# Fetching cache pages with direct transfers on SP's queue, addressed from registers, in place of indirect transfers on POOL's

## The chip, the cores and the metric

The kernel runs on one core of one Trainium2 chip. The metric is the device time of one execution in microseconds (us). A core has five engines that run side by side, each through its own queue of instructions in order: PE (TensorE, matrix products; its weight loads are shown as PEld), DVE (VectorE), ACT (ScalarE), POOL (GpSimd) and SP (SyncE, which here only issues transfers). All transfers run on the same 16 DMA engines.

## The reference, cut to what matters

One decoder layer serves a prompt (512 positions) and eight samples (8 new positions each, 1024 cached ones) with the same weights.

```python
z = rmsnorm(x) @ w_in                      # q, k/v streams, window k/v, gates, gMLP
# mixer A: three attention branches, gated and summed
kc, vc = compress_blocks(k_cmp), compress_blocks(v_cmp)   # a small MLP over blocks of 32 keys, stride 16
o = g0 * attend(q, kc, vc) + g1 * attend(q, selected 64-key blocks) + g2 * attend(q, last 512 keys)
# mixer B: u * (W_s v + b) in chunks of 128
x = x + [A ; B] @ w_out
x = x + relu(rmsnorm(x) @ w_ff1)**2 @ w_ff2
```

For the samples the past keys and values come out of a paged cache: `past = cache_kv[l][page_table]`. A page holds 128 positions; each sample has 8 pages, so the table has 64 entries, a permutation of pages in a pool of 80. Streams 0 and 1 (`k_cmp`, `v_cmp`) go into the compression, streams 2 and 3 into the selected-block branch.

## The kernel before, in words

The host lays the cache out as two arrays, `cache_kv` (compression streams) and `cache_slc` (selected streams), each with 128 rows of 256 floats per page: one page of either is 128 KB, one row of 1 KB for each of the 128 partitions.

The stages follow each other in the text of `_body`:

1. Norm and transposes of the input, then the whole projection by `w_in` for prompt and samples (`tok_mm`, `q_piece`), with the compression of the prompt's keys and the gMLP in between. The last projection product ends near 153 us, the gelu behind it near 170 us.
2. The prompt's attention (`prompt_attention`, lines 718 to 738): eight blocks of (key head, query tile), four heads each, so 32 steps. `head_scores` makes three score products per head and their maxima (DVE, line 672) and exponentials (ACT, line 673); `head_scales` normalises; `values` of the block before (transposes `tp`, line 703, copies `ptf`, products `o`) is interleaved. Beside it runs the compression of the samples' cached keys: from step 5 on, every third step, one of the eight tasks of lines 743 to 747 is emitted: `compress_keys(pr)` and `compress_values(pr)` for the four pairs of samples `pr`. Each calls `hidden`, 32 products of `w1` with the pages in `Gc[pr]`, written to `pcs`.
3. The samples' attention (`soft`, `values`, from line 777), which reads the pages in `Gs[pr]`, interleaved with the output projection (`out_proj`).
4. Norm, then the feed-forward layers over `w_ff1` and `w_ff2` (from line 1009) and the last norm.

The pages are fetched by `gather` (line 581): 16 pages for a pair of samples, one indirect transfer per page on POOL's queue, with row numbers out of `idx`, an integer tile made from the page table at lines 338 to 343 (table entry times 128 plus the partition's number). There are four fetches for `Gc` and four for `Gs`, 128 pages in all. `Gc` has two buffers (`gc_`, line 575), so `Gc[2]` and `Gc[3]` wait until the products on `Gc[0]` and `Gc[1]` are done; `load_cmp(pr + 2)` stands in `compress_values`, line 639. `Gs[0]` and `Gs[1]` have buffers of their own beside them; `Gs[2]` and `Gs[3]` (lines 768 to 770) take the place of `w1` and `Gc` once these are closed (line 749). The memory of all these tiles was the projection's, and comes free between 153 and 170 us.

SP issues every other load and store: in stage 2 the `VB` rows (577, 578), the window keys `KW` (595, two buffers), window values `W` (600) and `w1` (576); later the weights for the output projection and the feed-forward layers (`load_unit`, line 139).

The order on each engine's queue isn't that of the text alone. A scheduler simulates the program over time and puts each instruction on its engine's queue when its operands and its buffer are free in that simulation (line 1125, `schedule_with_timeline_sim`). On the chip a queue is then strictly in order: an instruction that waits holds all behind it on the same engine. In the trace POOL's order was 27 pages of `Gs[0]` and `Gs[1]`, then `Gc[0]` and `Gc[1]` whole, then the last 5 of `Gs[1]`, later `Gc[2]`, `Gc[3]`, `Gs[2]`, `Gs[3]`.

Of the kernel before, what the change touches and what calls it, by code (L numbers as in the profile page):

```python
# [11 lines left out]
F32 = mybir.dt.float32  # L12
F32R = mybir.dt.float32r
BF = mybir.dt.bfloat16
I32 = mybir.dt.int32
AF = mybir.ActivationFunctionType
ALU = mybir.AluOpType
# [14 lines left out]
def _build_consts():  # L32
    p = np.arange(128)
    blocks = []
    kept = ("ident", "gsum", "iota16", "valid0")

    def add(name, a):
        a = np.asarray(a, np.float32)
        full = np.zeros((128, a.shape[1]), np.float32)
        full[: a.shape[0]] = a  # L40
        blocks.append((name not in kept, name, full))

    add("ident", np.eye(128))
    add("causal", np.where(p[None, :] <= p[:, None], 0.0, NEG))
    n = np.arange(32)
    cm = [np.where(16 * n[None, :] + 31 <= (128 * i + p)[:, None], 0.0, NEG) for i in range(4)]
    add("cmpmask", np.concatenate(cm, 1))
    q = p % 8
    sm = np.zeros((128, 584), np.float32)
    sm[:, 63] = NEG  # L50
    sm[:, 64:72] = np.where(np.arange(8)[None, :] <= q[:, None], 0.0, NEG)
    c = np.arange(512)
    key = 4 * (c % 128) + c // 128
    sm[:, 72:] = np.where(key[None, :] >= q[:, None] + 1, 0.0, NEG)
    add("winmask", sm)
    add("newmask", np.where(np.arange(8)[None, :] <= q[:, None], 0.0, NEG))
    add("tril", (p[None, :] <= p[:, None]).astype(np.float32))
    seq, hh, gg = p // 64, (p % 64) // 32, (p % 32) // 8
    add("gsum", ((seq[:, None] == seq[None, :]) & (hh[:, None] == hh[None, :]) & (q[:, None] == q[None, :])))
    add("iota16", np.broadcast_to(np.arange(16), (128, 16)))  # L60
    add("headsel", ((hh * 4 + gg)[:, None] == np.arange(8)[None, :]))
    tok = np.arange(64)
    sel = [((tok // 8)[:, None] == (2 * pr + seq)[None, :]) & ((tok % 8)[:, None] == q[None, :]) for pr in range(4)]
    add("gatesel", np.concatenate(sel, 1))
    add("pageoff", p[:, None])
    add("rep8", (np.arange(8)[:, None] == (tok % 8)[None, :]))
    add("bdiag", (tok // 8)[:, None] == np.arange(8)[None, :])
    add("valid0", (p >= 31)[:, None])
    blocks.sort(key=lambda b: b[0])
    o = 0  # L70
    for _, name, a in blocks:
        _CONSTS[name] = (o, a.shape[1])
        o += a.shape[1]
    return np.concatenate([b[2] for b in blocks], 1), sum(b[2].shape[1] for b in blocks if not b[0])


CONST_ARRAY, NKEEP = _build_consts()
NCONST = CONST_ARRAY.shape[1]

# [5 lines left out]
def body(tc, I, O):  # L85
    nc = tc.nc
    ctx = ExitStack()
    with ctx:
        _body(ctx, tc, nc, I, O)


def _body(ctx, tc, nc, I, O):
    act, dve, pool, pe, sp = nc.scalar, nc.vector, nc.gpsimd, nc.tensor, nc.sync
# [22 lines left out]
    def C(name, rows=128):  # L116
        o, w = _CONSTS[name]
        return cst[:rows, o:o + w] if o < NKEEP else cst2_[0][:rows, o - NKEEP:o - NKEEP + w]
# [67 lines left out]
    samp = ctx.enter_context(tc.tile_pool(name="samp", bufs=1, side="right"))  # L186
# [4 lines left out]
    b2c = samp.tile([128, 2], F32, name="b2c")  # L191
    b2r = samp.tile([128, 2, 64], F32, name="b2r")
    b1p = samp.tile([128, 2, 2], F32, name="b1p")
    idx = samp.tile([128, 64], I32, name="idx")

    cot = ctx.enter_context(ExitStack())
    OTp = cot.enter_context(tc.tile_pool(name="otp", bufs=1, side="right")).tile([128, 8, NP], F32, name="OTp")
# [55 lines left out]
    early = ccs.enter_context(tc.tile_pool(name="early", bufs=1, side="right", reuse_waits="tile"))  # L253
# [54 lines left out]
    with ExitStack() as c4:  # L308
# [15 lines left out]
        for t in range(5):  # L324
            if t:
                norm_transpose(n1, pst, "tr", x[t][:tsz[t]], t, g1, AH, AL, AST)
            p = psm.tile([128, 512], F32, name="pd", tag="mm")
# [6 lines left out]
        pool.tensor_copy(dst, C(name))  # L334

    ptt = early.tile([128, 64], I32, name="ptt")
    pt = I["page_table"]
    sp.dma_start(ptt, bass.AP(tensor=pt.tensor, offset=pt.offset, ap=[[0, 128], [1, 64]]))  # L340
    ptf = early.tile([128, 64], F32, name="ptf")
    dve.tensor_copy(ptf, ptt)
    dve.tensor_scalar(idx, ptf, 128.0, C("pageoff"), op0=ALU.mult, op1=ALU.add)


    b1c = early.tile([128, 2], F32, name="b1c")
# [38 lines left out]
    for st in range(2):  # L385
        x_ = cp.tile([128, 8, 66], F32, name=f"X{st}")
        p = pst.tile([128, 512], F32, name="pkc", tag="tr")
# [41 lines left out]
    with ExitStack() as c4:  # L429
# [14 lines left out]
        for g2 in range(2):  # L444
            p = pst.tile([128, 4, 128], F32, name="pws", tag="tr")
# [12 lines left out]
        for t, p in enumerate(vps):  # L458
            rows = tsz[t]
            if t == 4:  # L460
                tmp = halves(p, 512)
                p = ev.tile([64, 512], F32, name="zg", tag="z")
# [8 lines left out]
                                     op0=ALU.subtract, op1=ALU.mult)  # L471
# [5 lines left out]
        p = pst.tile([128, 2, 64], F32, name="pkn", tag="tr")  # L477
# [4 lines left out]
        for g in range(0, 8, 2):  # L482
            p = pst.tile([128, 2, 4, 64], F32, name="psg", tag="tr")
# [4 lines left out]
        p = pst.tile([64, 8, 64], F32, name="psgs", tag="tr")  # L488
# [41 lines left out]
    for m in range(4):  # L530
        if m % 2 == 0:
            us = [load_pair(m * 128, i, pool) for i in range(4)]
        for half in range(2):
            p = psm.tile([128, 512], F32, name="pq", tag="mm")
# [5 lines left out]
    for t, p in enumerate(tok_mm(1304, 512)):  # L540
        rows = tsz[t]
        if t == 4:
# [3 lines left out]
            p = z  # L546
        u = uw.tile([128, 512], F32, name="u", tag="u", bufs=2)
        gelu(nc, uw, p, 512, None, None, out=u[:rows], rows=rows, times=S[:rows, t])
        p = pst.tile([128, 4, 128], F32, name="pob", tag="tr")
# [9 lines left out]
    with ExitStack() as c4:  # L559
# [20 lines left out]

        def gather(dst, src, pr):
            for j in range(16):
                pool.indirect_dma_start(out=dst[:, j], out_offset=None, in_=src,  # L583
                                        in_offset=bass.IndirectOffsetOnAxis(ap=idx[:, pr * 16 + j:pr * 16 + j + 1], axis=0))

        Gc = {}

        def load_cmp(pr):
            Gc[pr] = gc_[pr % 2].tile([128, 16, 256], F32, name="Gc", tag="Gc")
            gather(Gc[pr], I["cache_kv"], pr)  # L590
# [37 lines left out]
        def compress_values(pr):  # L628
            gel = hidden(pr, 1)
            pv = psf.tile([64, 2, 2, 64], F32, name="pv2", tag="fill")  # L630
            for sq in range(2):
                for h in range(2):
                    f = sq == 0 and h == 0
                    mm(pv[:, sq, h, :], gel[:, (h * 2 + sq) * 64:(h * 2 + sq) * 64 + 64], w2z[:, 1, 64:128],
                       f, True, f)
            dve.tensor_tensor(VB[0:64, pr].rearrange("p s (h d) -> p (s h) d", h=2),
                              pv.rearrange("p s h d -> p (s h) d"), bcast(b2r[0:64, 1], [[0, 4], [1, 64]]), op=ALU.add)
            if pr < 2:
                load_cmp(pr + 2)
            if pr == 1:  # L640
                gather(Gs[1], I["cache_slc"], 1)
# [98 lines left out]
        load_cmp(0)  # L740
        load_cmp(1)
        gather(Gs[0], I["cache_slc"], 0)
        tasks = [(f, pr) for pr in range(4) for f in (compress_keys, compress_values)]
        for i, _ in enumerate(prompt_attention()):
            if i >= 5 and i % 3 == 2 and tasks:
                f, pr = tasks.pop(0)
# [382 lines left out]
```

## Time and profile before

| | us |
|---|---|
| median of 3 runs | 998.38 (997.47 to 1001.69) |
| the profiled execution's own time | 999.24 |
| its span in the trace | 997.5 |

| engine | busy us | share of the span |
|---|---|---|
| PE | 833.1 | 84% |
| PEld | 688.7 | 69% |
| DVE | 429.8 | 43% |
| ACT | 344.8 | 35% |
| POOL | 228.6 | 23% |

The DMA engines moved 90.2 MB: 72.55 MB on the hardware queue (SP's transfers, 23.2% of the 16 engines' span) and 16.85 MB on the software queue (POOL's, 5.8%). The mean granted TensorE clock was 0.906 of full speed.

How to read such a profile: a row of a group or of the timeline gives the engine, the line of the kernel, the operation, the tile written and the tiles read. The bracket behind it is the time for which the engine stood idle before, and what is inferred to have ended that: an instruction, a transfer, "issue" (the engine waited for nothing that the profile shows) or "remote", which is the same as "another core or an unknown queue" in the chain (a signal whose sender the profile doesn't show). The shares of busy time are averages over stages with different limits, so a change in one stage is read from that stage.

### The profile page before, as it was taken

The numbers are of one execution on the slowest core, as the hardware profiler recorded it, in microseconds if no ns is written. First come the engines' busy times: TensorE is split into PE (matmuls) and PEld (weight loads), VectorE is DVE, ScalarE is ACT, GpSimd is POOL, SyncE is SP. The second block draws the span as 40 slices with busy tenths as digits, with TensorE's granted clock in tenths as the row PEclk, the third lists the DMA queues.
The fourth block names the chain that finished last, engine by engine and source line by source line (L and its number), as shares of the span: only waits on it lengthen the run. The fifth ranks groups of instructions, "written<-read, shape, count | busy, mean of one in ns | idle before, by whom it ended". The sixth has DMA issues, their size and how long they took to land.

```text
span 997.5 us, 12581 instructions
## 1 busy us (share of the span) xinstructions
PE 833.1 (84%) x4743; PEld 688.7 (69%) x4743; DVE 429.8 (43%) x900; ACT 344.8 (35%) x818; POOL 228.6 (23%) x273
## 2 busy tenths in 40 slices
PE   6999995212998599155997989999999999999996
PEld 4789983101666376022765778999999999989895
DVE  5529625101523254045743755353534344444425
ACT  5516425101533254034432644242323232323223
POOL 1006506773052403710000111111111111111112
PEclk9999996555997799558998999999999999999999
DMA  7633314631021201312417623132222222222002
GB/s 247 180 112 88 81 43 132 195 104 56 1 69 37 63 1 38 105 48 73 149 54 235 196 95 108 62 96 74 95 74 94 77 85 85 85 85 85 11 2 95
DMA packets 50172, 90.20 MB, mean 90 GB/s; under 512 B 8736, under 2 KB 17920, under 8 KB 49984
## 3 DMA queue, kind: packets, MB, share of 16 engines
q1 hardware_dynamic: 43712, 72.55, 23.2%
q0 software_dynamic: 6400, 16.85, 5.8%
q8 instruction: 37, 0.61, 0.3%
q14 instruction: 23, 0.19, 0.1%
HBM read 85.12 MB, written 8.39 MB: 94 GB/s over the span
## 4 chain that ended last, share of the span: by engine, by line
PE 72%; another core or an unknown queue 9%; DVE 6%; DMA 5%; issue 4%; ACT 2%; POOL 1%; SPq 0%; POOLq 0%; DVEq 0%; ACTq 0%
PE acc L96 42%; PE pd L96 8%; PE pcs L96 6%; PE o L96 4%; PE s L96 3%; PE tp L703 3%; PE pq L96 2%; DMA raw<-in_w_in 2%; DMA raw<-in_w_out 1%; DMA raw<-in_w_ff 1%; PE pc L96 1%; DVE ptf L102 1%; DVE nm L672 1%; POOL wu L108 1%
## 5 line engine op out<-in xcount | busy, mean ns | idle before, releaser
L96 PE MATMUL acc<-Hh,wu 128*128 128x288 f32 x1024 | 205.6, 295 | 0.2 <-ACT Hh L107 0.2
L107 ACT ACTIVATE wu<-raw 128x512 fp32r<-128x512 f32 (+1 forms) x184 | 106.1, 615 | 187.0 <-PE acc L96 119.4
L96 PEld LDWEIGHTS acc<-Hh,wu 128*128 128x128 f32 x1024 | 164.7, 188 | 0.6 <-ACT Hh L107 0.4
L96 PE MATMUL acc<-wu,Fh 128*128 128x512 f32 x512 | 155.3, 389 | 0.0
L96 PE MATMUL acc<-Hl,wu 128*128 128x288 f32 x512 | 150.8, 295 | 0.0
L108 DVE TENSOR_TENSOR wu<-raw,wu 128x512 fp32r<-128x512 f32 x168 | 109.4, 686 | 70.3 <-ACT wu L107 69.9
L96 PEld LDWEIGHTS acc<-wu,Fh 128*128 128x128 f32 x512 | 95.8, 188 | 19.6
L96 PE MATMUL acc<-wu,Fl 128*128 128x512 f32 x256 | 97.1, 389 | 0.0
L96 PEld LDWEIGHTS acc<-Hl,wu 128*128 128x128 f32 x512 | 96.1, 188 | 0.4
L936 POOL TENSOR_TENSOR R<-atm,R 64x512 f32<-64x512 f32 x18 | 29.4, 1635 | 280.5 <-DVE atm L935 153.8
L583 POOL DMA_INDIRECT Gs<-in_cache_slc,idx x64 | 62.0, 969 | 107.9 <-issue 70.3
L673 ACT ACTIVATE P<-s,nm 128x32 f32<-128x32 f32 (+4 forms) x88 | 40.1, 461 | 124.5 <-DVE nm L672 61.3
L672 DVE TENSOR_REDUCE nm<-s 128x1 f32<-128x32 f32 (+4 forms) x88 | 33.8, 403 | 107.1 <-remote 51.6
L583 POOL DMA_INDIRECT Gc<-in_cache_kv,idx x64 | 60.5, 945 | 80.8 <-PE pcs L96 61.9
L96 PE MATMUL pd<-wu,AH 128*128 128x512 f32 (+1 forms) x256 | 76.2, 380 | 0.3 <-POOL wu L108 0.2
L1027 DVE TENSOR_TENSOR f<-relu 128x576 f32<-128x576 f32 x32 | 24.2, 756 | 121.2 <-ACT relu L1026 121.2
L930 DVE TENSOR_TENSOR OTp<-acc,OTp 128x512 f32<-128x512 f32 x72 | 47.7, 687 | 53.8 <-PE acc L96 53.8
L1026 ACT ACTIVATE relu<-acc 128x288 f32<-128x288 f32 x64 | 26.1, 408 | 122.1 <-PE acc L96 122.1
L1029 POOL CAST Fst<-Fh 128x64 fp32r<-128x64 f32 x32 | 22.0, 687 | 180.1 <-ACT Fh L107 123.5
L96 PE MATMUL pcs<-Gc,w 128*128 128x256 f32 x256 | 60.0, 389 | 0.0
L96 PEld LDWEIGHTS acc<-wu,Fl 128*128 128x128 f32 x256 | 48.1, 188 | 10.0
L703 PEld LDWEIGHTS tp<-cst,P 128*128 128x128 f32 (+1 forms) x192 | 22.4, 146 | 45.8 <-issue 43.8
(311 smaller groups left out, 1310.5 us busy)
## 6 DMA issues: line engine op xcount, KB each, us to landing
raw<-in_w_ff SPq DMA_DIRECT2D x128, 256.0 KB, 3.3
raw<-in_w_in SPq DMA_DIRECT2D x32, 256.0 KB, 3.8
raw<-in_w_out SPq DMA_DIRECT2D x16, 256.0 KB, 6.1
out_wins<-in_state_win_kv SPq DMA_DIRECT2D x8, 504.0 KB, 5.7
KW<-in_win_kt SPq DMA_DIRECT2D x4, 512.0 KB, 3.6
W<-in_state_win_kv SPq DMA_DIRECT2D x8, 256.0 KB
OTp<-in_x_prompt SPq DMA_DIRECT2D x4, 512.0 KB
x<-in_x_prompt SPq DMA_DIRECT2D x3, 512.0 KB, 7.7
```

Source lines behind the costliest of these rows:

```text
L96: pe.matmul(out, lhsT, rhs, start=start, stop=stop, skip_group_check=not first_in_bank)
L107: act.activation(hi, src, AF.Copy)
L108: eng.tensor_tensor(lo, src, hi.bitcast(F32), op=ALU.subtract)
L583: pool.indirect_dma_start(out=dst[:, j], out_offset=None, in_=src, in_offset=bass.IndirectOffsetOnAxis(ap=idx[:, pr * 16 + j:pr * 16 + j + ...
L672: dve.tensor_reduce(nm[:, br, g:g + 1], src, axis=AX, op=ALU.max, negate=True)
L673: act.activation(p_[:, c0:c0 + w], src, AF.Exp, bias=nm[:, br, g:g + 1], accum_out=l[:, br, g:g + 1])
L703: pe.transpose(t_[:w, b, g * 128:(g + 1) * 128], P[g][:, c0:c0 + w], ident)
L930: dve.tensor_tensor(R[t][:, c0:c0 + 512], p, R[t][:, c0:c0 + 512], op=ALU.add)
L936: pool.tensor_tensor(R[4][:, c0:c0 + 512], tm2, R[4][:, c0:c0 + 512], op=ALU.add)
L1026: act.activation(r[:, i * 288:i * 288 + 288], p[:, :288], AF.Relu)
L1027: dve.tensor_tensor(f2, r, r, op=ALU.mult)
L1029: pool.tensor_copy(Fst[:, m, 0:64], Fh[:, m, 512:576].bitcast(F32))
```

## The change

The fetches are issued by SP as direct transfers of one page each. The page table is loaded as 64 integers into one partition. For every eight pages, one load brings eight entries of the table into registers of SP (`page`, with `j % 8 == 0`); a page's address is such a register times 128 rows. The tiles `idx` and `ptf`, the two DVE instructions that made `idx`, and the constant `pageoff` go. Buffers, sizes, the places of the calls to `gather` and everything that reads the pages are the same.

```diff
-    add("pageoff", p[:, None])
...
-    idx = samp.tile([128, 64], I32, name="idx")
...
-    ptt = early.tile([128, 64], I32, name="ptt")
-    pt = I["page_table"]
-    sp.dma_start(ptt, bass.AP(tensor=pt.tensor, offset=pt.offset, ap=[[0, 128], [1, 64]]))
-    ptf = early.tile([128, 64], F32, name="ptf")
-    dve.tensor_copy(ptf, ptt)
-    dve.tensor_scalar(idx, ptf, 128.0, C("pageoff"), op0=ALU.mult, op1=ALU.add)
+    ptt = samp.tile([1, 64], I32, name="ptt")
+    sp.dma_start(ptt, I["page_table"].rearrange("b n -> (b n)").unsqueeze(0))
+
+    pages = {}
+
+    def page(src, pr, j):
+
+        n = pr * 16 + j
+        if j % 8 == 0:
+            pages[0] = nc.values_load_multi_w_load_instructions(
+                ptt[0:1, n:n + 8], engines=[mybir.EngineType.SP], min_val=0, max_val=src.shape[0] // 128 - 1,
+                skip_runtime_bounds_check_because="the table holds numbers of pages of the pool alone")[1]
+        return src[bass.ds(pages[0][j % 8] * 128, 128), :]
...
         def gather(dst, src, pr):
             for j in range(16):
-                pool.indirect_dma_start(out=dst[:, j], out_offset=None, in_=src,
-                                        in_offset=bass.IndirectOffsetOnAxis(ap=idx[:, pr * 16 + j:pr * 16 + j + 1], axis=0))
+                sp.dma_start(dst[:, j], page(src, pr, j))
```

## Prediction

> **What bounds the kernel now.** I read the page first, for the clock and the chain that ended last.
>
> ```profile
> span 997.5 us, 12581 instructions
> PEclk9999996555997799558998999999999999999999
> PE 72%; another core or an unknown queue 9%; DVE 6%; DMA 5%; issue 4%; ACT 2%; POOL 1%; SPq 0%; POOLq 0%; DVEq 0%; ACTq 0%
> ```
>
> PE carries 72% of the chain. Unusual for one core: 9% hangs on a sender that isn't shown, and 4% is "issue". PEclk falls to 0.5 in slices 7 to 10, 13 and 17 (about 150 to 250, 300 to 330, 400 to 430 us), so PE has little to do there. Next, the busy time by stretches of that stage, the prompt's attention:
>
> ```profile
> core 0: us, PE busy (x) PEld busy (x) DVE busy (x) ACT busy (x) POOL busy (x), PEclk, DMA share, GB/s
> 177.00:250.00 73.00, 12.18 (x47) 7.84 (x45) 7.86 (x28) 8.61 (x33) 44.67 (x48) 0.50 0.37 111
> 250.00:263.00 13.00, 11.44 (x63) 6.30 (x61) 7.74 (x26) 7.74 (x26) 0.00 (x0) 0.86 0.00 0
> 296.00:305.00 9.00, 3.85 (x14) 2.02 (x13) 0.28 (x1) 0.79 (x2) 4.00 (x5) 0.62 0.27 81
> 332.00:341.00 9.00, 0.00 (x0) 0.00 (x0) 1.39 (x5) 1.46 (x4) 4.01 (x5) 0.70 0.26 79
> 397.00:433.00 36.00, 6.82 (x35) 3.37 (x35) 1.83 (x3) 0.38 (x2) 23.67 (x26) 0.60 0.33 95
> 433.00:444.00 11.00, 7.87 (x25) 3.49 (x25) 8.63 (x34) 8.08 (x33) 0.00 (x0) 0.50 0.14 49
> ```
>
> In four stretches, 73 + 9 + 9 + 36 = 127 us, nobody computes, and DMA is at about a third. Only POOL works, on its page fetches. In 250 to 263, without fetches, the same kind of work keeps PE at 11.44 of 13 us. Who waits? The waits of 165 to 263 and of 395 to 440, then the timeline:
>
> ```profile
> DVE nm L672 <- remote: 50.7, 8, 10.1
> DVE ptf L102 <- remote: 26.2, 1, 26.2
> ```
>
> ```profile
> 177.20 0.33 PE L96 MATMUL s<-causb,identb 128*128 128x128 bf16 x1
> 189.09 0.56 DVE L672 TENSOR_REDUCE nm<-s 128x1 f32<-128x384 f32 x1 [5.81 <-remote]
> 412.04 0.17 PE L96 MATMUL w_b<-kTn,qz 128*64 128x8 f32 x1 [1.70 <-issue]
> 413.43 0.17 PE L96 MATMUL w_b<-kTn,qz 128*64 128x8 f32 x1 [1.22 <-issue]
> 414.83 0.18 PEld L96 LDWEIGHTS w_b<-kTn,qz 128*64 128x64 f32 x1 [2.60 <-issue]
> ```
>
> The scores that DVE reduces at 189.09 were finished at 177.5, and DVE stood for 5.81 us with its operand ready. PE takes 1.4 us from one tiny product to the next, waiting for nothing shown. So no chain of operands is late; the engines start their instructions slowly. When? The first and last fetch of each run on POOL:
>
> ```profile
> 154.74 1.39 POOL L583 DMA_INDIRECT Gs<-in_cache_slc,idx  x1 [37.58 <-PE pd L96]
> 235.04 0.95 POOL L583 DMA_INDIRECT Gs<-in_cache_slc,idx  x1 [0.30 <-issue]
> 281.54 0.94 POOL L583 DMA_INDIRECT Gc<-in_cache_kv,idx  x1 [45.55 <-PE pcs L96]
> 300.28 0.95 POOL L583 DMA_INDIRECT Gc<-in_cache_kv,idx  x1 [0.30 <-issue]
> 317.55 0.95 POOL L583 DMA_INDIRECT Gc<-in_cache_kv,idx  x1 [16.32 <-PE pcs L96]
> 336.28 0.95 POOL L583 DMA_INDIRECT Gc<-in_cache_kv,idx  x1 [0.30 <-issue]
> 388.61 0.94 POOL L583 DMA_INDIRECT Gs<-in_cache_slc,idx  x1 [51.38 <-issue]
> 427.34 0.95 POOL L583 DMA_INDIRECT Gs<-in_cache_slc,idx  x1 [0.30 <-issue]
> ```
>
> Fetches go out every 0.95 + 0.30 = 1.25 us. Each slow stretch begins 8 to 22 us into such a run (397 − 388.6 and 177 − 154.7 are the ends) and closes 3 to 5 us behind its last fetch (the first, 14 us behind). Is it the traffic or the software queue? Compare a stretch with more traffic, all of SP's (first two rows), with the software queue in 405 to 432 (last row):
>
> ```profile
> 40.00:80.00 40.00, 40.00 (x218) 34.09 (x218) 16.60 (x34) 16.42 (x34) 3.44 (x5) 1.00 0.41 117
> q1 hardware_dynamic: 4254, 4.62, 40.6%
> q0 software_dynamic: 960, 2.62, 33.7%
> ```
>
> SP's queue at 40.6% and 4254 packets in 40 us leaves PE busy for 40.00 of 40 us. The software queue at 33.7% and 960 packets in 27 us brings PE almost to a halt. I conclude that the stage is bound by what POOL's indirect fetches do to the other engines, not by data that come late.
>
> **The change, part by part.** *Removed: 128 fetches on POOL, and the slow stretches.* What stays of each stretch is its own work, at the pace of 250 to 263 (13 us for 63 PE and 26 ACT instructions). 177 to 250: 33 ACT instructions, 33/26 × 13 = 16.5 us, saved 56.5. 296 to 305: 14 PE, 3 us, saved 6. 332 to 341: a few DVE and ACT instructions, 2 us, saved 7. 397 to 433: 35 PE, 7 us, saved 29. Sum 98.5. The clock: 433 to 444 runs at 0.50 behind a stall, and PE's 7.87 us there would be 3.9 at full clock; I take 4 (0 to 8, as other stretches behind a stall run slowly too). What is late next is PE itself. The 28.5 us left as work are a ceiling: PE's own part at full clock is 12.18 × 0.50 + 3.85 × 0.62 + 6.82 × 0.60 = 12.6, 15.9 less, if all else hides beside it.
>
> The SBUF — State Buffer page of the Trainium skill, "Who interferes with whom", speaks against this term: there a reduction on DVE never contends with GpSimd on this chip, and PE and ACT never wait on anyone. By that rule alone no stall would go, and the time would stay. The rows above differ on PE, which stood still in exactly these runs of fetches; I go by the rows.
>
> *Moved to SP: 128 transfers, 16 loads of eight registers, the address arithmetic.* The trace has no transfer with a register address. SP's rows:
>
> ```profile
> 155.52 0.29 SPq L578 DMA_DIRECT2D VB<-out_kvs  x1
> 169.24 0.73 SPq L576 DMA_DIRECT2D w<-in_cmp_w  x1
> 170.02 9.42 SPq L595 DMA_DIRECT2D KW<-in_win_kt  x1
> 529.50 5.10 SPq L895 DMA_DIRECT2D out_wins<-in_state_win_kv  x8
> KW<-in_win_kt SPq DMA_DIRECT2D x4, 512.0 KB, 3.6
> SPq L595 <- remote: 254.6, 1, 254.6
> ```
>
> Below: 0.29 us per page, a plain issue. Above: the 1.25 of POOL. I take 0.7, a little over the 5.10/8 = 0.64 of `out_wins`, since arithmetic and an eighth of a register load come on top. A lower price gains nothing more, as the pages are then early anyway. SP has room: after the `KW` issue that ends at 179.4 it waits 254.6 us for one buffer. Who needs the pages, and when:
>
> ```profile
> 263.38 6.96 PE pcs L96 x32
> 320.49 3.65 PE pcs L96 x16
> 362.94 3.65 PE pcs L96 x16
> 503.38 1.00 PE s__3456 L96 x2
> ```
>
> The first user of `Gc[0]` stands at 263.38; less 56.5, PE is there at 206.9. If SP takes all 32 pages of `Gs[0]` and `Gs[1]` first, then `w1` and `KW` (169.24 to 179.44, 10.2 us), then `Gc[0]`, it lands at 154.7 + 32 × 0.7 + 10.2 + 16 × 0.7 + 3.6 = 202.1: no wait, but a margin of 5 us only. At 1.25 per page it is 228.5, a wait of 22. `Gc[2]` starts at 281.54 − 56.5 = 225.0 and is needed at 320.49 − 62.5 = 258.0; 16 × 0.7 + 3.6 = 15 (at 1.25: 24) fit. `Gc[3]`: 255.1 to 293.4, fits. `Gs[2]`, `Gs[3]`: from 388.61 − 69.5 = 319.1, 32 × 0.7 = 22 us, needed at 503.38 − 98.5 = 404.9. Term: 0 (0 to 22).
>
> *A wait added on SP.* SP now holds for `Gc`'s buffers as POOL did, 45.55 and 16.32 us; behind it stand the third `KW` load, issued at 434.06 today, and the weights of the output projection, none of them needed within the stage. The register loads wait for the page table, 140 us early.
>
> *Removed: making `idx`.*
>
> ```profile
> L343 DVE TENSOR_SCALAR idx<-ptf,cst x1: 254/254/254, 20.0 to 20.0; 128x64 int32<-128x64 f32 x1
> ```
>
> Two small DVE instructions near 20 us, whose only readers are the fetches at 154 us; nothing.
>
> Sum: 999.24 − 98.5 − 4 + 0 = 896.7 for an execution like the profiled one; the runs' median lies 0.9 lower, so 896.
>
> **The rivals.** *The traffic does it, whoever issues.* For it: the slow stretches need 8 to 22 us of fetches before they begin, like a backlog, and at 170.02 SP's own issue took 9.42 us among them. Against it: 40 to 80. If the slowness lasts as long as the fetches, 98.5 + 4 shrink by 0.7/1.25: 45 saved, 954. If SP paces them at 1.25 too, or the stretches have nothing to do with the fetches, nothing is saved: 999, no change. The same comes out of the rule of the SBUF page above, and of Trainium Kernel Development and Optimization of the Trainium skill, "Key Constraints": the issuing queues share the 16 DMA engines, and issuing from several saves only the issue time.
>
> *SP becomes the bound (slower).* SP brings 101 pages before the work on `Gc[3]`: with c per page that work starts at 169 + 101c, and 444 − 98.5 − 4 − 293.4 = 48 us of the stage follow. It ends later than today's 444 from c = (444 − 169 − 48)/101 = 2.25 us on. At c = 2.5 the stage ends at 469.5: 1025. For it: no row prices a register load that holds SP eight pages long; 9.42 shows that one issue can be that dear. Against it: every issue into a free queue is between 0.29 and 0.73.
>
> **How the numbers follow.** Forecast, 896: 0.78. Its own range: 999.2 − 98.5 − 8 − 15.9 = 877 (only PE's own part left, clock up) to 999 − 98.5 + 22 = 923. Traffic with faster issue, 954: 0.09. No change, 999: 0.06. SP as bound, 1025: 0.07. To hold 8 in 10 I reach from 877 up to the 954. About 0.5%, 5 us, is what a measurement can tell from no change: faster 0.87, same 0.06, slower 0.07.
>
> **What would show it.** Right: no DMA_INDIRECT on POOL, the software queue nearly empty; the maxima of line 672 with no "remote" waits of 5 us and more; PE products in the stage 0.2 to 0.5 us apart; clock 1.0 from 200 us on; `pcs` near 207; the samples' attention starting a hundred us earlier; from 580 us of today on, the same lengths. The price per page is the spacing of SP's rows. Wrong: tiny products 1.4 us apart while SP's pages come in (traffic), or PE standing at `pcs` for a `Gc` transfer with SP busy without a gap (SP).

## The result, and the profile after

| | before | after | ratio (95%) |
|---|---|---|---|
| first measurement (4 executions each) | 1000.04 (997.47 to 1002.26) | 887.55 (883.79 to 888.97) | 0.887 [0.8833, 0.8908] |
| both measured again, on another chip or occasion (14 and 5) | 891.08 (889.35 to 893.08) | 887.53 (885.46 to 888.62) | 0.9953 [0.9936, 0.997] |

The forecast was 896. But one sentence has to stand ahead of all that follows: the kernel before took about 1000 us only in the first measurement; in 54 later executions, on four chips, it took between 887.2 and 894.3, while the changed kernel took the same 887.5 on both occasions. On which chip the first measurement ran isn't shown, nor whether both kernels ran on the same one there. So the change took 112 us away in the first measurement and 3.5 us in the second, and both have to be explained.

The page of the changed kernel, from the first measurement: span, clock, chain of waits and the two data queues (packets, MB, share of the 16 engines).

```profile
span 885.7 us, 12834 instructions
PEclk9999999669999988899998999999999999999998
PE 80%; DMA 7%; DVE 6%; ACT 2%; issue 2%; POOL 1%; SPq 1%; POOLq 0%; DVEq 0%; ACTq 0%
q1 hardware_dynamic: 62002, 89.30, 32.6%
q0 software_dynamic: 256, 0.07, 0.0%
```

The 9% of "another core or an unknown queue" are gone, and the software queue has only 0.07 MB left. Busy time by stretches, and the waits of 150 to 350 us (total, times, longest):

```profile
177.00:190.00 13.00, 7.33 (x32) 5.20 (x32) 6.96 (x27) 7.77 (x33) 0.00 (x0) 0.50 0.82 251
190.00:250.00 60.00, 58.04 (x300) 43.22 (x300) 23.21 (x74) 26.46 (x84) 0.00 (x0) 0.93 0.39 114
250.00:263.00 13.00, 13.00 (x73) 9.36 (x72) 6.69 (x23) 6.41 (x18) 0.00 (x0) 1.00 0.70 207
```

```profile
DVE nm L675 <- PE s L95: 46.3, 19, 14.8
PE pcs L95 <- DMA Gc<-in_cache_kv: 5.4, 1, 5.4
```

PE has 58.04 busy us in the 60 from 190 on. The maxima now wait for a sender that the profile shows: PE's scores. (46.3 us of DVE's time, which isn't the bound.) One transfer is waited for, 5.4 us for the first `Gc` page set. SP's queue, and PE where it meets the pages:

```profile
170.47 6.30 SPq L598 DMA_DIRECT2D KW<-in_win_kt  x1
177.85 20.29 SPq L587 DMA_DIRECT2D Gc<-in_cache_kv  x32
198.91 9.66 SPq L587 DMA_DIRECT2D Gs<-in_cache_slc  x16
```

```profile
184.33 0.63 PE L706 MATMUL tp<-cst,P 128*32 128x128 f32 x2
190.33 2.05 PE L95 MATMUL pcs<-Gc,w 128*128 128x256 f32 x4 [5.37 <-DMA Gc<-in_cache_kv]
```

A page costs SP 20.29/32 = 0.63 or 9.66/16 = 0.60 us. `Gc[0]` stands behind `KW`: 177.85 + 16 × 0.63 + 2.1 us of landing is 190.0, where `pcs` starts.

### The profile page after: what moved, and what is told of

Its sections match the earlier page's. It is cut to its first block, busy times and chain, and to the rows that moved or that the text cites. A ratio compares the mean times of both kernels' runs of the same rounds, so it can differ in the third digit from the quotient of the medians.

```text
span 885.7 us, 12834 instructions
## 1 busy us (share of the span) xinstructions
PE 820.1 (93%) x4743; PEld 685.0 (77%) x4743; DVE 428.2 (48%) x898; ACT 343.5 (39%) x818; POOL 106.3 (12%) x145
## 4 chain that ended last, share of the span: by engine, by line
PE 80%; DMA 7%; DVE 6%; ACT 2%; issue 2%; POOL 1%; SPq 1%; POOLq 0%; DVEq 0%; ACTq 0%
PE acc L95 48%; PE pd L95 9%; PE pcs L95 7%; PE o L95 4%; PE pq L95 3%; PE tp L706 3%; PE s L95 2%; DMA KW<-in_win_kt 1%; DMA raw<-in_w_out 1%; DMA raw<-in_w_ff 1%; DMA raw<-in_w_in 1%; PE pc L95 1%; DMA out_wins<-in_state_win_kv 1%; POOL wu L107 1%; DVE wu L107 1%
## 5 line engine op out<-in xcount | busy, mean ns | idle before, releaser
L95 PE MATMUL pcs<-Gc,w 128*128 128x256 f32 x256 | 62.6, 397 | 5.4 <-DMA Gc<-in_cache_kv 5.4
L95 PEld LDWEIGHTS pcs<-Gc,w 128*128 128x128 f32 x256 | 49.3, 199 | 14.9 <-issue 8.3
L675 DVE TENSOR_REDUCE nm<-s 128x1 f32<-128x32 f32 (+4 forms) x88 | 33.0, 402 | 54.7 <-PE s L95 46.3
L95 PEld LDWEIGHTS pd<-wu,AH 128*128 128x128 f32 x256 | 46.1, 191 | 9.4 <-DVE wu L107 0.5
L95 PE MATMUL acc<-wu,Hh 128*128 128x512 f32 x128 | 44.3, 421 | 5.3 <-ACT wu L106 5.0
L95 PE MATMUL pd<-wu,AL 128*128 128x512 f32 (+1 forms) x128 | 46.9, 372 | 0.0
```

The costliest lines, as they stand in the source:

```text
L95: pe.matmul(out, lhsT, rhs, start=start, stop=stop, skip_group_check=not first_in_bank)
L675: dve.tensor_reduce(nm[:, br, g:g + 1], src, axis=AX, op=ALU.max, negate=True)
```

## The experiments

The theory on record (A) says that POOL's indirect fetches slow the instruction starts of the other engines. The first five runs put fetches into a stage in which the changed kernel has none. They ran where the kernel before takes about 891 us (890.35 beside four of them, 891.60 beside the fifth), so they can show what fetches do there, not what they do where it took 1000.

**Fetches beside the feed-forward layers.** Four kernels add page fetches to the changed kernel in the feed-forward layers, into a scratch tile that nothing reads, 64 each: indirect ones on POOL, the same with rows of 128 bytes, direct ones with constant addresses on SP, and on POOL. A fifth adds 8 indirect ones. Those with indirect fetches also make `idx` again; the diff shows the fetches alone, of the first kernel.

```diff
+    scr = fp.tile([128, 4, 256], F32, name="scr")
...
+            if c == 2 and m == 0:
+                dve.tensor_copy(scr[:, :, 0], f2[:, 0:4])
+                for j in range(64):
+                    pool.indirect_dma_start(out=scr[:, j % 4], out_offset=None, in_=I["cache_kv"],
+                                            in_offset=bass.IndirectOffsetOnAxis(ap=idx[:, j:j + 1], axis=0))
```

> The changed kernel with 64 of the old fetches (indirect, POOL's queue, 128 rows of 1 KB each) put beside the feed-forward products of the third chunk, into four slots of a scratch tile that nobody reads. Theory A (POOL's indirect fetches slow the instruction starts of the other engines): 64 fetches at 1.25 us are 80 us; from some 8 to 22 us after the first to a few us after the last, PE's products stand 0.7 us and more apart, and the time is 50 to 70 us over the changed kernel's 888, 940 to 955. Rival (the old stage was slow since its pages came late or its order was bad): nobody waits for these fetches, so 888 within 5. Rival (traffic): as A, but then the same from SP's queue, by its time in flight.

> 64 indirect fetches of 128 rows on POOL's queue as in the first, but with rows of 128 bytes: the same number of rows, an eighth of the bytes. If the number of fetches and rows counts (theory A): still 50 to 70 us, 935 to 955. If the bytes count: an eighth of it, 888 to 900.

> The same 64 pages into the same four slots, as direct transfers on SP's queue with constant page numbers. Theory A: PE's products stay at their pace; SP's own weight loads come later by 64 x 0.33 to 0.63 = 21 to 40 us, most of which the weights loaded ahead cover: 888 to 905. Rival (traffic, whoever issues): slow while the pages are in flight, PE at 0.7 us per product for 20 to 40 us: 905 to 930.

> The same 64 pages as direct transfers on POOL's queue with constant page numbers: software queue, but no list of row numbers. If the software queue itself does it: as the indirect fetches, 940 to 955. If only the indirect form does: 888 within 8.

> Only 8 indirect fetches (10 us) beside the feed-forward products. If the slowness needs a backlog (in the old kernel it began 8 to 22 us into a run): 888 within 3. If each fetch costs the engines its share at once: 8/64 of the cost of the run of 64, 7 to 9 us: 895 to 897.

Measured, one execution each: 894.00, 892.18, 890.52, 886.16 and 884.98. The 64 indirect fetches, first and last on POOL; busy time meanwhile; and PE's only wait there:

```profile
581.88 1.07 POOL L1043 DMA_INDIRECT scr<-in_cache_kv,idx  x1 [7.69 <-DVE scr L1041]
671.32 0.95 POOL L1043 DMA_INDIRECT scr<-in_cache_kv,idx  x1 [0.30 <-issue]
```

```profile
582.00:671.00 89.00, 84.27 (x489) 76.04 (x488) 39.86 (x59) 26.99 (x52) 71.47 (x81) 0.98 0.55 173
```

```profile
PE acc L96 <- POOL Fst L1047: 4.7, 1, 4.7
```

For 89 us the fetches go out at the pace of the first profile, 1.25 us each with POOL's other work between, and PE is busy for 84.27 of 89 us; what it lacks is one wait of 4.7 us for POOL's own cast `Fst`, which stood behind the fetches on POOL's queue. That is a queue in order, not a slow start of PE. With the 64 transfers on SP instead, in 100 us around them, PE stays busy too (and with direct ones on POOL for 100.00 of the same 100):

```profile
580.00:680.00 100.00, 99.27 (x586) 89.91 (x585) 45.52 (x69) 30.89 (x59) 14.68 (x20) 1.00 0.53 163
```

So, on these chips, neither the indirect form nor the traffic of the pages makes a slow stretch by itself. The rival of the traffic falls there, and theory A holds at most under some further condition. With the short rows the time, 892.18, lies in the range that was given for "the bytes count"; since full rows made no slow stretch either, it doesn't show that.

**Half of the fetches back on POOL, in their old place.** `Gs` is fetched by indirect transfers again, `Gc` by SP.

```diff
-                sp.dma_start(dst[:, j], page(src, pr, j))
+                if src is I["cache_kv"]:
+                    sp.dma_start(dst[:, j], page(src, pr, j))
+                else:
+                    pool.indirect_dma_start(out=dst[:, j], out_offset=None, in_=src,
+                                            in_offset=bass.IndirectOffsetOnAxis(ap=idx[:, pr * 16 + j:pr * 16 + j + 1], axis=0))
```

> Half of the change undone: the Gs pages are fetched by POOL's indirect transfers again, the Gc pages by SP as in the changed kernel. Theory A: the two runs of 32 fetches stay (the first from about 155 us, the second before the samples' attention), each with a slow stretch that begins 8 to 22 us into it: some 20 to 30 us lost each, 930 to 950. Rival (late pages bound the old stage): Gc is early, Gs has a hundred us of room, so 888 within 5.

Measured: 891.03, where the kernel before took 891.60 (889.03 to 893.26). The fetches of `Gs[0]` and `Gs[1]` begin at 154.72 and run on beyond 190, as before, yet:

```profile
154.72 1.38 POOL L598 DMA_INDIRECT Gs<-in_cache_slc,idx  x1 [37.58 <-PE pd L96]
190.09 0.95 POOL L598 DMA_INDIRECT Gs<-in_cache_slc,idx  x1 [0.30 <-issue]
```

```profile
177.00:190.00 13.00, 11.48 (x47) 7.78 (x45) 7.30 (x27) 7.73 (x33) 9.73 (x11) 0.50 1.03 326
```

PE issues 47 instructions in 177 to 190, in the midst of the fetches. The slow stretch isn't there. Theory A, which expected 930 to 950, misses by 39 us or more.

**The two kernels unchanged, again.** After these misses the premise itself had to be tried.

> The kernel before, unchanged, on this chip. Theory A (the slow stretches belong to the program: with all 128 fetches on GpSimd's software queue the starts of the other engines fall on a coarse grid at 177 to 250, 296 to 305, 332 to 341 and 397 to 433 us): 990 to 1005 us again, with TensorE busy well below 90% in the windows 177:250 and 397:433. Rival D (they belong to the chip, or to where the buffers and the code came to lie in the runs shown, and the program only gives the occasion): 885 to 900 us here, TensorE busy above 90% in those windows, though the 128 fetches still run.

> The changed kernel, unchanged, on the same chip. Both theories expect 883 to 892 us. Theory A: a ratio to the kernel before of 0.88 to 0.89. Rival D: a ratio of 0.98 to 1.005, since without the slow stretches the change has only the 5 to 10 us of the prompt's compression waits to win.

Measured: before 891.11 (890.19 to 894.32), after 887.53; the reference runs of the kernel before beside them 891.08. The page of the kernel before, its span, clock, chain and software queue; then the two longest stretches of the prediction and the one between them without stalls; then POOL's first fetches and PE at `pcs`:

```profile
span 889.0 us, 12581 instructions
PEclk9999999567999998899699999999999999999999
PE 79%; DVE 7%; DMA 6%; POOL 3%; ACT 3%; issue 2%; SPq 0%; POOLq 0%; DVEq 0%; ACTq 0%
q0 software_dynamic: 6400, 16.85, 6.5%
```

```profile
177.00:250.00 73.00, 61.00 (x299) 43.30 (x298) 30.56 (x99) 32.74 (x112) 55.43 (x58) 0.81 0.45 132
250.00:263.00 13.00, 12.86 (x72) 10.36 (x72) 5.61 (x21) 6.07 (x17) 9.62 (x11) 1.00 0.36 102
...
397.00:433.00 36.00, 30.70 (x258) 21.84 (x254) 18.39 (x65) 12.60 (x40) 0.00 (x0) 0.90 0.41 134
```

```profile
155.39 1.38 POOL L583 DMA_INDIRECT Gs<-in_cache_slc,idx  x1 [37.56 <-PE pd L96]
190.74 0.94 POOL L583 DMA_INDIRECT Gc<-in_cache_kv,idx  x1 [0.30 <-PE tp L703]
212.34 9.80 PE L96 MATMUL pcs<-Gc,w 128*128 128x256 f32 x32 [8.65 <-DMA Gc<-in_cache_kv,idx]
```

The same 12581 instructions, the same 16.85 MB on the software queue, POOL's fetches in the same order and at the same 1.25 us each; but in 177 to 250 PE issues 299 instructions, where the first profile had 47, and no part of the chain hangs on an unknown sender. The slow stretches aren't a property of the program. Rival D is right as far as that; what in the first measurement made them isn't told apart by any run.

The two traces show more of what was late. Engines tell each other that a result is ready by raising a counter (a semaphore), and a trace holds such raises with their times. In the first profile the scores that DVE reduces at 189.09 end at 177.53, but the raise of PE's counter is recorded at 189.07, and DVE starts 0.02 us later. So DVE did not start slowly there: the signal came 11.5 us after the product, and "remote" stands for such a raise, with no instruction ending near it. In and beside the slow stretches 30 raises of that counter are recorded 0.5 to 17 us after the end of the last instruction that makes one; `before_again` has none like that, apart from two at the very end, which both traces have. Records are also missing: of the raises that mark the landing of POOL's transfers the first trace holds 512, the other 2175 for the same transfers. In the fourth stretch PE's starts themselves are slow, in products that neither wait for a counter nor raise one (1.4 us apart at 412 to 415). Late signals, missing records and slow starts lie in the same stretches. What made them isn't shown; that the recording itself took part is a rival that no run tests.

**What the change is worth where the engines start evenly.** Two rows by stage and the span show where the profiled executions' 3.2 us (889.0 − 885.8) lie: the products of the output projection and of the feed-forward layers, each with its first and last start. Kernel before, then after:

```profile
L96 PE MATMUL acc<-wu,Hh x128: 387/392/796, 363.4 to 461.2; 128*128 128x512 f32 x128
L96 PE MATMUL acc<-Hh,wu x1024: 288/294/588, 471.1 to 855.7; 128*128 128x288 f32 x171
```

```profile
L95 PE MATMUL acc<-wu,Hh x128: 387/393/797, 355.8 to 453.7; 128*128 128x512 f32 x128
L95 PE MATMUL acc<-Hh,wu x1024: 290/294/607, 464.3 to 851.7; 128*128 128x288 f32 x171
```

The output projection begins 363.4 − 355.8 = 7.6 us earlier. The shorter wait at `pcs`, 5.3 in place of 8.6, is 3.3 of them; the rest isn't taken apart. The projections take 108.5 in place of 107.7 us, and the rest 885.8 − 464.3 = 421.5 in place of 417.9, so 0.8 + 3.6 are given back, and 3.2 remain. Why the feed-forward layers are longer shows in PE's timeline at their start, before and then after, and in the busy time and granted clock (third figure from the end) from the first product on, two rows of before and three of after:

```profile
469.13 0.66 PE L173 MATMUL ptr<-cst,xn 128*128 128x128 f32 x4 [3.53 <-DVE Hl L108]
470.33 1.11 PE L173 MATMUL ptr<-cst,xn 128*128 128x128 f32 x4 [0.55 <-DVE ms L146]
471.10 0.83 PE L96 MATMUL acc<-Hh,wu 128*128 128x288 f32 x2
```

```profile
462.54 1.97 PE L172 MATMUL ptr<-cst,xn 128*128 128x128 f32 x8 [4.33 <-DVE Hl L107]
464.34 0.85 PE L95 MATMUL acc<-Hh,wu 128*128 128x288 f32 x2
466.16 1.11 PE L172 MATMUL ptr<-cst,xn 128*128 128x128 f32 x4 [0.97 <-DVE Hl L107]
```

```profile
471.10:475.10 4.00, 4.00 (x23) 4.00 (x22) 3.08 (x5) 1.63 (x3) 0.75 (x2) 0.67 0.15 51
475.10:479.10 4.00, 4.00 (x34) 4.00 (x33) 1.48 (x3) 1.50 (x3) 0.00 (x0) 1.00 0.02 4
```

```profile
464.30:468.30 4.00, 3.03 (x13) 2.64 (x13) 3.28 (x5) 2.23 (x4) 0.54 (x1) 0.50 0.28 91
468.30:472.30 4.00, 4.00 (x22) 3.98 (x22) 1.05 (x2) 0.44 (x1) 0.00 (x0) 0.63 0.00 0
472.30:476.30 4.00, 4.00 (x32) 3.61 (x31) 1.12 (x2) 0.92 (x4) 0.00 (x0) 1.00 0.01 4
```

The scheduler, simulating another program, has put a transpose `ptr` behind the first products of the feed-forward layers; PE stands another 0.97 us there, and in the first 8 us its clock is at 0.50 and 0.63 and it issues 13 and 22 instructions; in the kernel before the clock was at 0.67 for the first 4 us and then at full speed, with 23 and 34. At the 32 per 4 us that follow, the 22 fewer are 2.75 us, an estimate; the products of these layers last 387.4 − 384.6 = 2.8 us longer, and the other 0.8 lie behind the last one. None of this was touched by the diff. That the moved `ptr` made the low clock is read from these rows; no run moves it back.

**The other half on POOL.** `Gc` by indirect transfers on POOL, `Gs` by SP (the condition of the edit above turned round).

```diff
-                if src is I["cache_kv"]:
+                if src is not I["cache_kv"]:
```

> The compression pages (Gc) are fetched by GpSimd's indirect transfers as before, the selected pages (Gs) by SP from registers. Theory W (where the engines start evenly, all that the change is worth is TensorE's wait for Gc[0], which in the kernel before stands behind 32 pages of Gs at 1.25 us each): Gc[0] now has nothing ahead of it, 16 pages at 1.25 us, so the wait falls from 8.6 us to under 3, and the time is 881 to 887 us where the kernel before takes 889 to 893. Rival V (indirect fetches cost the other engines some time on every chip, a little here and much where the profile before was taken): 888 us or more, as half of the fetches remain. If the kernel before takes about 1000 us in this call too, the slow state is met again, and this kernel tells whether the Gc half alone brings it: 930 to 960 us if so.

Measured: 890.28 (889.28 to 891.73), ratio 0.9992 [0.9978, 1.0006].

```profile
171.59 1.05 POOL L598 DMA_INDIRECT Gc<-in_cache_kv,idx  x1 [53.58 <-PE pob L563]
196.91 8.61 PE L96 MATMUL pcs<-Gc,w 128*128 128x256 f32 x32 [4.09 <-DMA Gc<-in_cache_kv,idx]
```

```profile
L96 PE MATMUL acc<-wu,Hh x128: 387/393/797, 356.9 to 455.6; 128*128 128x512 f32 x128
L96 PE MATMUL acc<-Hh,wu x1024: 288/294/606, 466.2 to 853.5; 128*128 128x288 f32 x171
```

Theory W (881 to 887) got the time wrong. The wait fell from 8.6 to 4.1, not below 3, since `Gc`'s buffer comes free at 171.6 only; and of the 363.4 − 356.9 = 6.5 us won in the stage, 1.6 went in the projections (466.2 − 356.9 = 109.3) and 4.9 from the start of the feed-forward layers on (889.0 − 466.2 = 422.8). The wait alone doesn't set the time. (`gs_on_pool` has almost the same rows, with starts at 357.0 and 466.6.)

Rival V, by which indirect fetches cost some time on every chip, asked for 888 or more, and the time is there. The 4.9 us lost from 466.2 on can't be its price, as no page is fetched so late. But a small price fits the stage itself: from the first score product (170.3 to 172.7 us) to the output projection, less the wait at `pcs`, it takes 183.2 us with 128 indirect fetches (`before_again`), 181.0 here and 181.4 in `gs_on_pool` with 64, and 176.0 to 180.4 in the ten runs with none there (178.9 in `after_again`). That would be 3 to 7 us for all 128, an estimate. The order on the queues differs between the kernels too, so V is neither shown nor ruled out.

**Who issues, and where the addresses come from.** The direct transfers on POOL's queue, with the registers loaded there; and SP's transfers with fixed pages in place of the table's, so that other pages are read.

```diff
-                ptt[0:1, n:n + 8], engines=[mybir.EngineType.SP], min_val=0, max_val=src.shape[0] // 128 - 1,
+                ptt[0:1, n:n + 8], engines=[mybir.EngineType.Pool], min_val=0, max_val=src.shape[0] // 128 - 1,
...
-                sp.dma_start(dst[:, j], page(src, pr, j))
+                pool.dma_start(dst[:, j], page(src, pr, j))
```

```diff
-                sp.dma_start(dst[:, j], page(src, pr, j))
+                sp.dma_start(dst[:, j], src[(pr * 16 + j) * 128:(pr * 16 + j + 1) * 128, :])
```

> The changed kernel's direct transfers with addresses in registers, but on POOL's queue. If only the indirect form slows the engines: 888 to 900, the difference being POOL's pace per page. If any transfer of the software queue does: 960 to 1000.

> The changed kernel with constant page numbers in place of the table's (other pages are read): SP's transfers alone, no register loads, no address arithmetic. The trace of the changed kernel has 0.63 us per page, of which 0.33 is the transfer's own row. Expected: 0.35 to 0.45 us per page, the first 16 Gc pages some 3 us earlier, PE's wait for them (5.4 us) down to 2 to 3: 884 to 887. Rival (register price bounds the stage): more than 10 us gained, below 878.

> The changed kernel with its 128 direct transfers, their addresses in registers, on GpSimd's queue in place of SP's, timed in rounds. It has no wait of TensorE for Gc[0], since KW no longer stands ahead of it, and Gs no longer ahead as in the kernel before. Theory W' (on chips where the engines start evenly the change is worth what the prompt's attention and the compression gain, less the 3 us given back where the feed-forward layers begin): 882 to 885 us, a ratio of 0.990 to 0.994 to the kernel before at 889 to 893. Rival (any page fetch on GpSimd's queue costs the other engines): 888 or more. If the kernel before takes about 1000 us in this call, the slow state is met, and this kernel tells whether GpSimd's queue (about 1000 again) or the indirect form of the transfers (about 884) brings it.

Measured: POOL with registers 883.66, and, in a second run with five executions, 881.08 (879.90 to 883.28), ratio to the kernel before 0.9896 [0.9878, 0.9915]; SP with fixed pages 883.46 (882.43 to 884.38), 0.9905 [0.9881, 0.9929]. The second run of POOL with registers: its software queue, its pages, PE at `pcs`, and the two starts.

```profile
q0 software_dynamic: 6400, 16.85, 6.5%
```

```profile
171.34 4.71 POOL L587 DMA_DIRECT2D Gc<-in_cache_kv  x8 [53.59 <-PE pob L555]
180.00 0.55 POOL L587 DMA_DIRECT2D Gc<-in_cache_kv  x1 [0.17 <-issue]
192.17 7.34 PE L95 MATMUL pcs<-Gc,w 128*128 128x256 f32 x32
```

```profile
L95 PE MATMUL acc<-wu,Hh x128: 387/392/797, 349.7 to 447.6; 128*128 128x512 f32 x128
L95 PE MATMUL acc<-Hh,wu x1024: 288/294/607, 458.0 to 845.7; 128*128 128x288 f32 x171
```

A page costs POOL 4.71/8 = 0.59 us in the first row and 0.55 + 0.17 = 0.72 in the second, `pcs` has no wait, and the stage ends 13.7 us earlier than in the kernel before (363.4 − 349.7); 0.6 and 3.0 are given back (458.0 − 349.7 = 108.3, and 878.9 − 458.0 = 420.9), 10.1 us remain. This version is the fastest of the three, below the 882 to 885 that were expected. It moves the same 6400 packets over the software queue as the kernel before. The Trainium skill, DMA: Bandwidth & Descriptors, section "SWDGE vs HWDGE vs iDMA", says that GpSimd's direct transfers go through its software descriptors just as the indirect ones do; the packet count agrees. So on these chips direct transfers on that queue cost the other engines nothing that the times show, and the rivals that asked for 888 or more (960 in the first run) fall.

SP with fixed pages came out just under the 884 to 887 expected, but its wait at `pcs` is 4.1 us, not 2 to 3, and SP's order is another one: 14 pages of `Gs` ahead of `Gc`, and `KW` behind it, at 195.5. So this run doesn't price the registers alone. That they bound the stage, which asked for less than 878, falls.

## Why the prediction was right, and where it was not

**What bounds the kernel: failed as a statement about the program.** "I conclude that the stage is bound by what POOL's indirect fetches do to the other engines" rests on one place of measurement. The fetches run as before in `before_again`, beside the feed-forward layers and, by halves, in `gs_on_pool` and `gc_on_pool`, and no slow stretch appears. For the first measurement it stays true that the slow stretches lay in the runs of fetches and that the changed kernel, without these, has none; but that the one made the other was not shown. The reading "DVE stood for 5.81 us with its operand ready" is wrong as it stands: the operand was ready, but the signal for it is recorded only 0.02 us before the start. The profile held two hints. The waits named no sender ("remote") where the kernel has one, PE's scores. And the first fetches, from 154.74 to 177, went out while the engines still started normally, so fetches alone were not enough even there.

**The saving, 98.5 + 4.** In the first measurement the output projection began at 471.7 before and at 355.7 after, 116.0 us earlier, against 102.5 forecast. `before_again`, which has no slow stretches, begins it at 363.4: so 471.7 − 363.4 = 108.3 us is what the stretches cost, 5.8 more than forecast and within the 15.9 that the prediction named as what would go if their remaining work hid beside PE's. The other 7.7 are what the change is worth without them, and the sum had no term for those.

**SP's pages, 0 (0 to 22).** The price was near: 0.60 to 0.63 for 0.7. The order was not: SP took `KW` and then `Gc[0]`, not `Gs` first, and PE's queue has the compression earlier, at 190 and not at 207. A wait of 5.4 us came of it, inside the bounds. It is the sign that the prediction gave for SP as the bound, for these 5.4 us; PE waits for no other page of SP's.

**"The same lengths" later on.** They are not: from the first feed-forward product to the end it took 417.3 us before (580.2 to 997.5) and 421.4 after (464.3 to 885.7). That fits the moved `ptr` and the clock behind it. With the 116.0 and 0.1 in the projections (108.5 and 108.6) it gives 111.8, the difference of the two spans.

**The rivals.** "No change, 999", at 0.06, is nearest to what the second measurement shows, a change of 3.5 us, though not at 999: there the fetches go on and nothing is slow. The prediction had this outcome also from the Trainium skill, SBUF — State Buffer, "Who interferes with whom", by whose rule on shared memory ports PE and ACT never wait on anyone. The later runs agree with that rule: 47 instructions of PE in 13 us beside POOL's fetches in `gs_on_pool`, and 84.27 of 89 us busy in `ffn_indirect64`. The prediction set it aside for one profile's rows. For the first measurement the forecast of 896 was right in sign and within 9 us; the mechanism that it gave was not confirmed. That it came so near is in good part luck: the sum priced the end of the slow stretches, and whether the change ended them, or the changed kernel ran where there were none, isn't shown.

**What stays open.** Whether the chip, the place of buffers or code in memory, the recording, or something else at work beside the kernel made the first measurement slow; and whether the fetches took part. It isn't shown that the kernel before was ever run again where it had been slow, and none of its later executions took more than 894.3 us. Whether indirect fetches cost the prompt's stage a few us on the other chips stays open too.

## What to carry to other kernels

A stall for which the profile shows no sender, and in which ready instructions start late, can belong to the run and not to the program: measure the kernel before again elsewhere before building a sum on it, and compare the time at which a signal is recorded with the end of the work that it reports. Where a change moves pages from one queue to another, look at what stands ahead of the first page that someone needs; here POOL's version pays about the same per page as SP's, starts `Gc` at 171.3 in place of 177.9, and was 6.5 us faster (881.08 and 887.53); how much of that is the order alone, the runs don't separate. And follow the saving to the end of the kernel: the stages behind the attention gave back 3.6 to 6.5 us of it, far from the edit.

## What the runs showed of the hardware

- One program of 12581 instructions took 997 to 1002 us in five executions (the profiled one, 999.24, among them) and 887 to 894 in 54 others; in the first profile's longest slow stretch PE issued 47 instructions in 73 us, in the later one 299 in the same window.
- In those stretches a counter that PE raises is recorded up to 17 us after the product that it reports (11.5 us for the scores reduced at 189.09), and DVE started 0.02 us behind it; in the later trace no raise of it is more than 0.5 us late, apart from two at the very end.
- A page of 128 KB costs its issuer 0.60 to 0.63 us on SP with the address in a register, 0.59 to 0.72 on POOL in that form, and 1.25 on POOL as an indirect transfer.
- After pauses of PE of 4.33 and 0.97 us the granted clock stood at 0.50 and 0.63 for 8 us, with 13 and 22 instructions; after pauses of 3.53 and 0.55 us it stood at 0.67 and 1.00, with 23 and 34.
